# Six gated-map buffers for five, eleven kept gelu results for thirteen, and the second U block split at the end of the score stage

## The chip, the cores and the metric

The kernel runs on one core of a Trainium2 chip. The metric is the device time of one execution in microseconds (us). TensorE is PE (its weight loads PEld), VectorE DVE, ScalarE ACT, GpSimd POOL, SyncE SP.

## What is computed

Two layers, each a token mixer followed by a PEER expert layer; the change lies in the expert layer. For every token and each of 8 heads, 16 of 16384 experts are picked by product keys, and the output is the sum of their V rows, weighted by gelu of the token's product with their U row, times a softmax gate.

```python
def peer_ffn(xn, wq, sub_keys, u_tab, v_tab):
    q = jnp.matmul(xt, wq).reshape(t, PEER_HEADS, 2, PEER_SUBDIM)
    scores = jnp.einsum('thcd,hcnd->thcn', q, sub_keys)
    sv, si = lax.top_k(scores, PEER_TOPK)
    ...
    best_s, best_p = lax.top_k(cand_s, PEER_TOPK)
    gate = jax.nn.softmax(best_s, axis=-1)
    ...
        act = jnp.einsum('td,thkd->thk', xb, u_tab[ib])
        wgt = jax.nn.gelu(act) * gb
        return jnp.einsum('thk,thkd->td', wgt, v_tab[ib])
```

## The kernel before

Of the 512 tokens, 384 are computed densely: U is cut into 128 blocks of 128 experts, and all products of a block with the 384 tokens are made on PE. The last 128 tokens take their rows by indirect DMAs on POOL (`gather`, one row per token and step, followed by one multiply on DVE, L743 or L754).

A U block `e` passes these steps: `uload` (DMA of 512 KB into one of three `u_raw`), `uprep` (ACT rounds it to the upper half `u_hi`, L688), `uprep_lo` (DVE subtracts to get the lower half `u_lo`, L682; three buffers of each half), and `uact` (24 matmuls, L714, of which the first two of a block need only `u_hi` and the third needs `u_lo`; then gelu on ACT, L717). `act_st` holds `NB` gelu results; the first `NS` = 60 blocks are stored to memory (`ge`), the others stay in `act_st` until the V loop uses them.

The expert layer of a layer runs in these stages; the times are those of the first layer (the second is alike, 1611.6 us later).

- **Score stage** (to 443 us): queries and key scores; its instructions are put in order by the scheduler of the framework. At its end `uprep(0)` splits U block 0.
- **Top-k stage** (448 to 574 us, `stage2`): DVE picks the 16 best of each token tile, in four tiles. From here on the code's order is the order on each engine, but for work that the scheduler finds free. `credit(0.8)` at every `yield` lets U blocks in: each whole credit emits one `uphase(e)`, which puts `u_lo` of block e+1 on DVE, `u_hi` of e+2 on ACT and the 24 matmuls of e on PE. After each tile PE transposes its indices (L868, L869).
- **Map stage** (589 to 825 us): gates are put in place by one-hot products, in 24 batches of 16 tokens. `make_maps(b, step)` makes a batch on DVE: step 0 two equality maps `oeq` (L900, two buffers), steps 1 to 3 one gated map `oag` each (L905, `AGB` buffers; a batch uses three). `quad(b, b4)` is 12 matmuls on PE (L918) that need all five maps, then ACT moves the result to `st` (L920); every eight quads `st` is stored (L922). Order of issue: quad (b, 0..3), each followed by one step of batch b+1, `credit(0.38)`, and after every third quad a gather. U blocks stop at `pace["e"] == UB - 4`, where `UB = NS + NB - 3`: at 66.
- **Seven U blocks alone** (825 to 856 us; `u_tail` = 66 to 72), with matmul banks of a new pool.
- **V loop** (856 to 1612 us): for each of 128 blocks V is split as U was, `wh`/`wl` are gelu times gate, and 18 matmuls (L1011) are added up; the U blocks left (55) are spread over the first 120 steps, and most gathers run here.

Of the kernel before, what the change touches and what calls it, by code (L numbers as in the profile page):

```python
# [41 lines left out]
NCH = TD // TC  # L42
GE = 4
GPAD = 128
NB = 13
NS = 60
UB = NS + NB - 3
W_S = 0.8
W_O = 0.38
G_R = 1  # L50
AGB = 5
UR = 3
G_B = 1
GBUF = 4
# [15 lines left out]
def trunk_kernel(ctx: ExitStack, tc: tile.TileContext, x, norm1_g, w_in, sb_qn_g, sb_kn_g, ml_conv_w,  # L70
# [598 lines left out]
    def layer(l):  # L669
        with ExitStack() as pctx:  # L670
            pools = {}
            uraw, uT, vraw, vT, wT, g4 = {}, {}, {}, {}, {}, {}

            def uload(e):
                if e < NK:
                    uraw[e] = pools["up"].tile([P, ND, P], F32, name="u_raw", bufs=UR)
                    nc.sync.dma_start(uraw[e], peer_ut[l, e])

            def uprep_lo(e):
                if e in uraw:  # L680
                    src = uraw.pop(e)
                    nc.vector.tensor_sub(uT[e][1], src, uT[e][0].bitcast(F32))  # L682

            def uprep(e, lo=True):
                if e < NK:
                    uh = pools["up"].tile([P, ND, P], F32R, name="u_hi", bufs=3)
                    ul = pools["up"].tile([P, ND, P], F32R, name="u_lo", bufs=3)
                    nc.scalar.activation(uh, uraw[e], AF.Copy)  # L688
                    uT[e] = (uh, ul)
                    if lo:  # L690
                        uprep_lo(e)

            with ExitStack() as fctx:
                ps = fctx.enter_context(tc.tile_pool(name="ps_f", bufs=1, space=PSUM))
                wst = fctx.enter_context(tc.tile_pool(name="wst", bufs=1))
                mctx = ExitStack()
                fr = mctx.enter_context(tc.tile_pool(name="fr", bufs=1))
                at = mctx.enter_context(tc.tile_pool(name="at", bufs=1))
                mixing(l, wst, fr, at, ps)
                pr, xg, sbuf, svs, sis = peer_front(l, pctx, mctx, at, wst, ps, pools, uload)  # L700
                uprep(0)
            dr = pctx.enter_context(tc.tile_pool(name="dr", bufs=1, space=bass.MemoryType.DRAM))
            gd = dr.tile([NCH, P, NK * TC + GPAD], F32, name="gd")
            ge = dr.tile([NS, P, TD], F32, name="ge")
            gb = pctx.enter_context(tc.tile_pool(name="gb", bufs=GBUF - 2))
            act_st = pctx.enter_context(tc.tile_pool(name="act_st", bufs=NB))
            gelu = {}
# [13 lines left out]
            def uphase(e, ps):  # L721
                uprep_lo(e + 1)
                uload(e + 4)
                uprep(e + 2, lo=False)
                uact(e, ps)
# [34 lines left out]
            def gather(n):  # L760
                for f, p in [todo.pop() for _ in range(min(n, len(todo)))]:
                    f(p)
# [8 lines left out]
            with ExitStack() as bctx:  # L771
# [117 lines left out]
                def pairs(row, b):  # L889
                    row = row[:, b * OT:(b + 1) * OT].rearrange("p (q b) -> p q b", b=2)  # L890
                    return row[:, :, None, :].to_broadcast(QS)

                def make_maps(b, step):
                    if b >= n_bat:
                        return
                    if step == 0:
                        eq = oh.tile([P, 2] + QS[1:], BF16, name="oeq")
                        maps[b] = (eq, [])
                        for i in range(2):
                            nc.vector.tensor_tensor(eq[:, i], iota_t[:, None].to_broadcast(QS), pairs(idxT[:, i], b),  # L900
                                                    op=ALU.is_equal)
                    else:
                        eq, ag = maps[b]
                        ag.append(oh.tile(QS, BF16, name="oag", bufs=AGB))
                        nc.vector.tensor_mul(ag[-1], eq[:, 0], pairs(gateT[:, step - 1], b))  # L905

                def quad(b, b4):
                    c, o = divmod(b * OT, TC)
                    o += b4 * 4
                    if o == 0:  # L910
                        sts[c] = stg.tile([P, NK, TC], F32, name="st")
                    st = sts[c]
                    eq, ag = maps[b]
                    pg = ps.tile([P, 4, NK], F32, name="oh", bufs=5)
                    for k in range(4):
                        q, r = divmod(b4 * 4 + k, 2)
                        for i in range(3):
                            nc.tensor.matmul(pg[:, k, :], eq[:, 1, q, :, r], ag[i][:, q, :, r],  # L918
                                             start=(i == 0), stop=(i == 2))
                    nc.scalar.activation(st[:, :, o:o + 4].rearrange("p i t -> p t i"), pg, AF.Copy)  # L920
                    if o + 4 == TC:
                        nc.scalar.dma_start(gd[c, :, :NK * TC], sts.pop(c).rearrange("p i t -> p (i t)"))  # L922
                    if b4 == QB - 1:
                        del maps[b]

                def credit(w):
                    pace["credit"] += w
                    while pace["credit"] >= 1 and pace["e"] < UB - 4:
                        uphase(pace["e"], ps)
                        pace["e"] += 1  # L930
                        pace["credit"] -= 1

                with tc.manual_schedule():
                    uprep(1, lo=False)
                    uload(3)
                    for t in (NT - 1, *range(NT - 1)):
                        for _ in stage2(t):
                            credit(W_S)
                    casts = [f() for f in late]
                    credit(W_S)  # L940
                    for f in casts:
                        f()
                    tkctx.close()
                    with ExitStack() as octx:
                        oh = octx.enter_context(tc.tile_pool(name="oh", bufs=2))
                        stg = octx.enter_context(tc.tile_pool(name="stg", bufs=2))
                        for step in range(4):
                            make_maps(0, step)
                            credit(W_O)
                        for b in range(n_bat):  # L950
                            for b4 in range(QB):
                                quad(b, b4)
                                make_maps(b + 1, b4)
                                credit(W_O)
                                gather((b * QB + b4) % 3 == 1)
                u_tail = pace["e"]

            with ExitStack() as cctx:
# [12 lines left out]
                def vload(k):  # L971
                    if k >= NK:
                        return
                    e = order[k]
                    if e < NS:
                        gelu[e] = vp.tile([P, TD], F32, name="gelu_r", bufs=3)
                        nc.sync.dma_start(gelu[e], ge[e])
                    if e % GE == 0:
                        g4[e // GE] = vp.tile([P, NCH, GE, TC], F32, name="gt4")
                        nc.sync.dma_start(g4[e // GE].rearrange("p c i t -> p c (i t)"),  # L980
                                          gd[:, :, e * TC:(e + GE) * TC].rearrange("c p f -> p c f"))
                    vraw[e] = vp.tile([P, D], F32, name="v_raw", bufs=3)
                    nc.sync.dma_start(vraw[e], peer_v[l, e * NK:(e + 1) * NK, :])
# [30 lines left out]
                with tc.manual_schedule():  # L1014
# [11 lines left out]
                    for k in range(NK):  # L1026
                        u_on = eu < NK and (k + 1) * (NK - NS - NB) >= (eu - NS - NB + 1) * UEND
                        vload(k + 2)
# [15 lines left out]
    for l in range(depth):  # L1044
        layer(l)
# [36 lines left out]
```

## Time and profile before

| | |
|---|---|
| runs, us | 3225.39, 3228.98 (median), 3235.2 |
| profiled execution, us | 3232.74, of which the span 3231.0 |
| busy in the span | PE 96%, PEld 86%, DVE 78%, ACT 43%, POOL 21% |
| granted TensorE clock, mean | 0.986 of full speed |
| moved by DMA | 748.49 MB, 232 GB/s in the mean |

The span runs from the first to the last instruction; 1.7 us of the execution lie around it. PE is near its limit in every stage, so what matters are the stretches in which it stands still: 3231.0 - 3116.7 = 114.3 us in all.

### The profile page before, as it was taken

Reading aid. Unit: us, or ns where it says so; the run is one execution under the profiler, and the core shown is the slowest. Engines: PE = TensorE matmul, PEld = TensorE weight load, DVE = VectorE, ACT = ScalarE, POOL = GpSimd, SP = SyncE. Lnnn points to the kernel's source line nnn. Section 1 sums busy time; section 2 is a strip of 40 time slices with the busy share of each in tenths; the row PEclk is TensorE's granted clock in tenths of the full one; section 3 lists DMA queues with packets and bytes.
Section 4 is the critical chain, followed back from the end, with each engine's and each line's share of the span. In section 5 each row is a group of like instructions: output and inputs, shape, how many; then the busy total and the mean of one; then the engine's idle time right before and its main releaser. Section 6 shows DMA issues by size and latency. Waiting matters only on the chain.

```text
span 3231.0 us, 46311 instructions
## 1 busy us (share of the span) xinstructions
PE 3116.7 (96%) x17496; PEld 2776.7 (86%) x17496; DVE 2509.5 (78%) x4655; ACT 1388.0 (43%) x2002; POOL 681.5 (21%) x563
## 2 busy tenths in 40 slices
PE   8999999999999999999989999999999999999999
PEld 8877889998888888888887878899988888888888
DVE  4757889988677777877747578899886777778777
ACT  4553424566433333333355533345663333333333
POOL 1000000122233333333300000001212333333333
PEclk9999999999999999999999999999999999999999
DMA  4212325687999999999732123257879999999997
GB/s 141 68 33 61 102 70 176 232 291 264 337 331 324 324 332 316 334 330 323 252 107 67 34 60 101 75 186 242 289 262 322 328 329 321 332 318 336 328 324 264
DMA packets 329344, 748.49 MB, mean 232 GB/s; under 512 B 26404, under 2 KB 191328, under 8 KB 326048
## 3 DMA queue, kind: packets, MB, share of 16 engines
q1 hardware_dynamic: 233632, 401.76, 37.3%
q0 software_dynamic: 74752, 269.84, 23.9%
q10 hardware_dynamic: 20736, 73.93, 6.0%
q8 instruction: 137, 2.24, 0.3%
q14 instruction: 87, 0.71, 0.1%
HBM read 669.41 MB, written 76.02 MB: 231 GB/s over the span
## 4 chain that ended last, share of the span: by engine, by line
PE 85%; DVE 10%; ACT 3%; issue 2%; DMA 1%; SPq 0%; ACTq 0%; POOL 0%; DVEq 0%; POOLq 0%
PE y L1011 32%; PE act L714 26%; PE mm L187 13%; PE oh L918 4%; PE mm L533 3%; DVE u_lo L682 2%; DVE oag L905 1%; PE zz L367 1%; PE zz L653 1%; PE zz L467 1%; PE y L400 1%; PE y L478 1%; PE zz L392 1%; DVE bp L808 1%; DVE bp L805 1%
## 5 line engine op out<-in xcount | busy, mean ns | idle before, releaser
L714 PE MATMUL act<-xh,u_hi 128*128 128x384 f32 x2048 | 699.5, 342 | 6.4 <-ACT st L920 5.1
L714 PE MATMUL act<-xh,u_lo 128*128 128x384 f32 x2048 | 693.1, 338 | 11.2 <-DVE u_lo L682 11.2
L714 PE MATMUL act<-xl,u_hi 128*128 128x384 f32 x2048 | 693.0, 338 | 0.0
L1011 PE MATMUL y<-v_hi,wh 128*128 128x512 f32 x1536 | 599.9, 391 | 3.9 <-ACT wh L998 3.9
L1011 PE MATMUL y<-v_lo,wh 128*128 128x512 f32 x1536 | 599.6, 390 | 0.7 <-DVE v_lo L999 0.7
L1011 PE MATMUL y<-v_hi,wl 128*128 128x512 f32 x1536 | 598.7, 390 | 0.0
L997 ACT ACTIVATE v_hi<-v_raw 128x1024 fp32r<-128x1024 f32 x256 | 272.0, 1063 | 648.0 <-issue 575.5
L682 DVE TENSOR_TENSOR u_lo<-u_raw,u_hi 128x1024 fp32r<-128x1024 f32 x256 | 312.3, 1220 | 182.8 <-ACT u_hi L688 182.7
L999 DVE TENSOR_TENSOR v_lo<-v_raw,v_hi 128x1024 fp32r<-128x1024 f32 x256 | 312.9, 1222 | 160.8 <-ACT v_hi L997 160.8
L714 PEld LDWEIGHTS act<-xh,u_lo 128*128 128x128 f32 x2048 | 387.3, 189 | 13.6 <-DVE u_lo L682 13.3
L714 PEld LDWEIGHTS act<-xh,u_hi 128*128 128x128 f32 x2048 | 387.4, 189 | 11.4 <-ACT st L920 5.4
L714 PEld LDWEIGHTS act<-xl,u_hi 128*128 128x128 f32 x2048 | 387.2, 189 | 4.1
L740 POOL DMA_INDIRECT sbuf<-in_peer_u_dram,idx x128 | 170.8, 1334 | 1012.8 <-DVE sbuf L743 482.1
L717 ACT ACTIVATE gelu<-act 128x384 f32<-128x384 f32 x256 | 126.1, 492 | 521.7 <-PE act L714 521.6
L1011 PEld LDWEIGHTS y<-v_hi,wl 128*128 128x128 f32 x1536 | 289.2, 188 | 61.5 <-DVE wl L1000 0.7
L1011 PEld LDWEIGHTS y<-v_hi,wh 128*128 128x128 f32 x1536 | 288.8, 188 | 60.9 <-ACT wh L998 4.5
L1011 PEld LDWEIGHTS y<-v_lo,wh 128*128 128x128 f32 x1536 | 289.1, 188 | 57.0 <-DVE v_lo L999 1.3
L688 ACT ACTIVATE u_hi<-u_raw 128x1024 fp32r<-128x1024 f32 x256 | 271.7, 1062 | 37.0 <-ACT gelu L717 7.7
L740 POOL DMA_INDIRECT rows<-in_peer_u_dram,idx x128 | 165.5, 1293 | 365.9 <-DVE rows L743 354.1
L751 POOL DMA_INDIRECT sbuf<-in_peer_v_dram,idx x128 | 167.7, 1311 | 279.6 <-DVE x_sb L754 262.6
L920 ACT ACTIVATE st<-oh 128x512 f32<-128x512 f32 x192 | 198.6, 1141 | 46.6 <-PE oh L918 46.6
L751 POOL DMA_INDIRECT rows<-in_peer_v_dram,idx x128 | 159.3, 1245 | 280.0 <-DVE x_sb L754 246.4
(295 smaller groups left out, 5158.7 us busy)
## 6 DMA issues: line engine op xcount, KB each, us to landing
u_raw<-in_peer_ut_dram SPq DMA_DIRECT2D x256, 512.0 KB, 5.0
v_raw<-in_peer_v_dram SPq DMA_DIRECT2D x256, 512.0 KB, 6.5
gd<-st ACTq DMA_DIRECT2D x24, 2048.0 KB, 8.0
gt<-gd SPq DMA_DIRECT2D x64, 768.0 KB, 9.4
ge<-gelu ACTq DMA_DIRECT2D x120, 192.0 KB, 3.8
gelu_r<-ge SPq DMA_DIRECT2D x120, 192.0 KB, 6.1
w_raw<-in_w_in_dram SPq DMA_DIRECT2D x28, 768.0 KB, 4.4
w_raw<-in_peer_wq_dram SPq DMA_DIRECT2D x20, 768.0 KB, 5.5
```

What stands on the lines that cost most here:

```text
L187: nc.tensor.matmul(ps, a_sel(a[ah], d), b_sel(b[bh], d), start=(d == 0 and i == 0), stop=(d == n - 1 and i == 2))
L682: nc.vector.tensor_sub(uT[e][1], src, uT[e][0].bitcast(F32))
L688: nc.scalar.activation(uh, uraw[e], AF.Copy)
L714: nc.tensor.matmul(pa[:, :TD], a[:, d, :], b[:, d, :TD], start=(d == 0 and i == 0), stop=(d == ND - 1 and i == 2))
L717: nc.scalar.activation(gelu[e], pa[:, :TD], AF.Gelu_apprx_tanh)
L740: nc.gpsimd.indirect_dma_start(out=r, out_offset=None, in_=u_rows, in_offset=bass.IndirectOffsetOnAxis(ap=idx[:, p:p + 1], axis=0))
L751: nc.gpsimd.indirect_dma_start(out=r, out_offset=None, in_=v_rows, in_offset=bass.IndirectOffsetOnAxis(ap=idx[:, p:p + 1], axis=0))
L918: nc.tensor.matmul(pg[:, k, :], eq[:, 1, q, :, r], ag[i][:, q, :, r], start=(i == 0), stop=(i == 2))
L920: nc.scalar.activation(st[:, :, o:o + 4].rearrange("p i t -> p t i"), pg, AF.Copy)
L997: nc.scalar.activation(vh, vraw[e], AF.Copy)
L999: nc.vector.tensor_sub(vl, vraw.pop(e), vh.bitcast(F32))
L1011: nc.tensor.matmul(ya[2 * t + half], a[:, tsl], b[:, hs], start=(k == 0 and i == 0), stop=(k == NK - 1 and i == 2))
```

## The change

```diff
-NB = 13
+NB = 11
...
-AGB = 5
+AGB = 6
...
             def uprep_lo(e):
-                if e in uraw:
+                if e in uraw and e in uT:
...
                 pr, xg, sbuf, svs, sis = peer_front(l, pctx, mctx, at, wst, ps, pools, uload)
                 uprep(0)
+                uprep(1)
...
                 with tc.manual_schedule():
-                    uprep(1, lo=False)
                     uload(3)
```

A gated map takes 4 KB of a partition and a gelu result 1.5 KB. With `NB` = 11, `UB` is 68 for 70: U blocks in the map stage stop at 64, the seven alone are 64 to 70, and 57 stand in the V loop. The lower half of U block 1 is made in the score stage; the changed condition keeps `uphase(0)` from making it again. From line 702 to 934 the changed kernel's line numbers are one higher.

Three places show what moves. The first is DVE near the end of the norm that opens the score stage (`rs` is the row scale of a tile, `xg` the normed last tile, `xl` the lower half of its transpose), as a piece of the difference:

```order
 L682 TENSOR_TENSOR u_lo<-u_raw,u_hi 128x1024
 L151 SCALAR_TENSOR_TENSOR rs<-rq_b,rs 128x1
+L682 TENSOR_TENSOR u_lo<-u_raw,u_hi 128x1024
 L214 SCALAR_TENSOR_TENSOR xg<-x_sb,rs,sp 128x1024
 L203 TENSOR_TENSOR xl<-zz,xh 128x4x128
```

The lower half of block 1 now stands between the last row scale and `xg`. The second place is DVE in the first tile of the top-k stage (the searches of heads, `bs` and `bp` their values and places), before:

```order
L807 MAX bs<-c_3914 128x8
L808 MAX_INDEX bp<-bs,c_3914 128x8
L682 TENSOR_TENSOR u_lo<-u_raw,u_hi 128x1024
L804 MAX bs<-cand 128x8
L805 MAX_INDEX bp<-bs,cand 128x8
```

and now:

```order
L808 MAX bs<-c_3915 128x8
L809 MAX_INDEX bp<-bs,c_3915 128x8
L805 MAX bs<-cand 128x8
L806 MAX_INDEX bp<-bs,cand 128x8
L807 MATCH_REPLACE c_3954<-bs,cand 128x64
```

That lower half is gone from between the second and the third head; all later ones keep their places. The third place is the end of the map stage. On ACT each `st` row is one quad and each `gelu` one U block; the last rows of the first layer's map stage before:

```order
L920 ACTIVATE st<-oh 128x4x128 x3
L688 ACTIVATE u_hi<-u_raw 128x1024
L717 ACTIVATE gelu<-act 128x384
L920 ACTIVATE st<-oh 128x4x128
L922 DMA gd<-st 128x4096
L920 ACTIVATE st<-oh 128x4x128 x2
L688 ACTIVATE u_hi<-u_raw 128x1024
L717 ACTIVATE gelu<-act 128x384
L920 ACTIVATE st<-oh 128x4x128 x2
L688 ACTIVATE u_hi<-u_raw 128x1024 x2
L717 ACTIVATE gelu<-act 128x384
L920 ACTIVATE st<-oh 128x4x128 x4
```

and now:

```order
L921 ACTIVATE st<-oh 128x4x128 x3
L688 ACTIVATE u_hi<-u_raw 128x1024 x2
L718 ACTIVATE gelu<-act 128x384
L921 ACTIVATE st<-oh 128x4x128
L923 DMA gd<-st 128x4096
L921 ACTIVATE st<-oh 128x4x128 x8
L923 DMA gd<-st 128x4096
```

Four quads stood behind the last U block of the stage, and now nine do. On DVE the same place, with the last batch's maps, reads now:

```order
L906 TENSOR_TENSOR oag<-oeq,gateT 128x2048
L682 TENSOR_TENSOR u_lo<-u_raw,u_hi 128x1024
L901 TENSOR_TENSOR oeq<-iota_t,idxT 128x2048 x2
L744 SCALAR_TENSOR_TENSOR sbuf,act_g<-sbuf,xg 128x1024
L906 TENSOR_TENSOR oag<-oeq,gateT 128x2048 x3
L744 SCALAR_TENSOR_TENSOR rows,act_g<-rows,xg 128x1024 x2
```

The last batch's two equality maps, a gather's multiply and its three gated maps follow each other with no lower half between them.

## Rows read from the trace of the kernel before

**Rows 1.** The page, busy us (share of the span) xinstructions of each engine.
```profile
PE 3116.7 (96%) x17496; PEld 2776.7 (86%) x17496; DVE 2509.5 (78%) x4655; ACT 1388.0 (43%) x2002; POOL 681.5 (21%) x563
```
**Rows 2.** The page, the chain that ended last, shares by engine.
```profile
PE 85%; DVE 10%; ACT 3%; issue 2%; DMA 1%; SPq 0%; ACTq 0%; POOL 0%; DVEq 0%; POOLq 0%
```
**Rows 3.** Waits of PE, both layers: us in total, times, longest us.
```profile
PE oh L918 <- DVE oag L905: 32.2, 28, 1.9
PE act L714 <- DVE u_lo L682: 11.2, 6, 4.8
```
**Rows 4.** Stages: us, busy PE, PEld, DVE, ACT, POOL (xinstructions), PEclk, DMA, GB/s.
```profile
448.00:574.00 126.00, 118.00 (x654) 116.07 (x654) 120.56 (x417) 55.15 (x69) 4.06 (x4) 0.97 0.56 176
...
589.00:825.00 236.00, 217.88 (x1994) 210.37 (x1992) 208.41 (x215) 149.04 (x168) 52.65 (x33) 1.00 0.78 273
825.00:856.00 31.00, 29.39 (x168) 29.07 (x168) 14.69 (x19) 10.26 (x16) 5.87 (x7) 1.00 1.00 367
856.00:1612.00 756.00, 755.13 (x3623) 663.77 (x3624) 597.50 (x748) 271.46 (x365) 269.47 (x214) 1.00 0.92 319
```
**Rows 5.** Timeline of a batch's end: start, us, what [idle before <-releaser]; DVE.
```profile
635.23 1.23 DVE L905 TENSOR_TENSOR oag<-oeq,gateT 128x2048 bf16<-128x2048 bf16 x1 [2.05 <-PE oh L918]
...
637.52 2.36 DVE L900 TENSOR_TENSOR oeq<-iota_t,idxT 128x2048 bf16<-128x2048 bf16 x2
```
**Rows 6.** The same timeline, PE.
```profile
636.51 0.73 PE L918 MATMUL oh<-oag,oeq 128*128 128x128 bf16 x10 [1.09 <-DVE oag L905]
```
**Rows 7.** Map stage, DVE groups: xcount | busy us, mean ns | idle before, releaser.
```profile
L905 DVE TENSOR_TENSOR oag<-oeq,gateT 128x2048 bf16<-128x2048 bf16 x68 | 82.3, 1221 | 26.6 <-PE oh L918 26.6
L900 DVE TENSOR_TENSOR oeq<-iota_t,idxT 128x2048 bf16<-128x2048 bf16 x44 | 51.8, 1219 | 0.0
L682 DVE TENSOR_TENSOR u_lo<-u_raw,u_hi 128x1024 fp32r<-128x1024 f32 x37 | 45.0, 1219 | 0.0
L743 DVE SCALAR_TENSOR_TENSOR sbuf<-sbuf,xg 128x1024 f32<-128x1024 f32 x16 | 19.5, 1218 | 0.0
```
**Rows 8.** The chain that ended last, 440 to 600 us: start, us, what.
```profile
451.94 1.12 DVE u_lo L682
...
591.36 4.29 PE act L714 x24
```
**Rows 9.** End of the map stage on PE, in order of time.
```profile
820.03 2.93 PE L918 MATMUL oh<-oag,oeq 128*128 128x128 bf16 x48
825.19 0.44 PE L714 MATMUL act<-xh,u_hi 128*128 128x384 f32 x1 [2.23 <-ACT st L920]
```
**Rows 10.** Start of the top-k stage on PE.
```profile
453.12 0.69 PE L714 MATMUL act<-xh,u_lo 128*128 128x384 f32 x1 [4.79 <-DVE u_lo L682]
```
**Rows 11.** The second lower half of the top-k stage on DVE.
```profile
455.47 1.20 DVE L682 TENSOR_TENSOR u_lo<-u_raw,u_hi 128x1024 fp32r<-128x1024 f32 x1
```
**Rows 12.** End of the top-k stage on PE.
```profile
574.02 0.41 PE L868 MATMUL tr<-ident,ii 128*128 128x128 f32 x2 [1.62 <-DVE ii L852]
```
**Rows 13.** Waits of DVE from 443 to 596 us: us in total, times, longest.
```profile
DVE sbuf L661 <- ACT sc L656: 1.4, 1, 1.4
```
**Rows 14.** Score stage, the last tile's norm on DVE.
```profile
336.09 1.28 DVE L214 SCALAR_TENSOR_TENSOR xg<-x_sb,rs,sp 128x1024 f32<-128x1024 f32 x1
```
**Rows 15.** Score stage, its transposes on PE.
```profile
339.26 0.60 PE L199 MATMUL zz<-ident,xg 128*128 128x128 f32 x4
```
**Rows 16.** Stretches after PE stood still; columns as in Rows 4.
```profile
453.10:458.70 5.60, 5.58 (x17) 5.58 (x18) 5.22 (x31) 0.00 (x0) 0.00 (x0) 0.50 0.49 124
825.10:828.50 3.40, 3.31 (x19) 3.31 (x20) 0.00 (x0) 0.04 (x1) 0.07 (x1) 1.00 1.03 299
2346.40:2349.80 3.40, 3.40 (x18) 3.40 (x17) 3.40 (x4) 1.95 (x2) 0.65 (x1) 0.50 0.83 257
2438.50:2441.90 3.40, 3.40 (x13) 3.40 (x12) 0.00 (x0) 0.00 (x0) 0.00 (x0) 0.51 1.07 341
```
**Rows 17.** V loop, a PE group: columns as in Rows 7.
```profile
L1011 PE MATMUL y<-v_hi,wh 128*128 128x512 f32 x768 | 299.9, 391 | 1.9 <-ACT wh L998 1.9
```

## The prediction

> **What bounds the kernel now.** I read the page first. PE is busy for 96% of the span [rows 1], and the chain that ended last runs through PE for 85% of it and through DVE for 10% [rows 2]. So there is little to win but the stretches in which PE stands still, and a change can win only those that it touches. The waits of PE name two such: its one-hot products wait for gated maps of DVE, 32.2 us in 28 waits, 14 in each layer, and its U blocks wait for lower halves, 11.2 us in 6, the longest 4.8 [rows 3]. The table by stage then says who has room. In the map stage PE is busy for 217.88 of 236 us and DVE for 208.41; in the V loop PE is busy for 755.13 of 756 [rows 4], so a U block that is moved there takes its own time and no more, and none is gained. In the top-k stage DVE is busy for 120.56 of 126 us.
>
> **The sixth map buffer.** The timeline of one batch's end shows what it touches. DVE stands still for 2.05 us until PE has ended a quad, then makes a gated map in 1.23 us [rows 5]; PE, which has finished that quad, stands still for 1.09 us until this map is there [rows 6]. With five buffers a batch's third map takes the buffer of the first map of the batch before, which is read until that batch's last quad; so its multiply can start only when PE has nothing left but quads that need it. DVE has 26.6 us of idle time in the map stage, all of it before gated maps and waiting for PE, none before equality maps or lower halves [rows 7]. With six the third map takes a buffer that was free a batch earlier, and this wait of both is gone: 32.2/2 = 16.1 us per layer.
>
> What is late next is DVE itself. It starts operations 1.13 us apart (two equality maps take 2.36, one alone 1.22 [rows 5, 7]). A batch is five maps, 1.52 lower halves at 1.12 [rows 8] and 1.33 gathers at 1.22 [rows 7]: 5.65 + 1.7 + 1.6 = 9.0 us. On PE a batch is four quads, 2.93 us with the last one's run-out and 2.75 without [rows 9], and 1.52 U blocks of 4.29 [rows 8]: 9.3 us. So PE stays the longer by a little, but a batch with one U block is 7.0 us on PE and 8 to 9 on DVE, and the lead that DVE may have is one batch, since equality maps have two buffers. The longest of the 14 waits is 1.9 us [rows 3], 0.8 above the common 1.09: there DVE was late by itself. I leave two waits of 1 us in each layer, 2.0 us; the bounds are none and half of the 16.1.
>
> **Eleven gelu results.** U blocks in the map stage end at 64 for 66, and nine quads stand behind the last one for four. While the last batch but one is in the quads, DVE has to make the last batch's maps, and cannot start before quad 3 of the batch ahead of it is done, because the two equality maps are in use till then. DVE then needs five maps and a gather's multiply, 5 x 1.13 + 1.22 = 6.9 us; PE has four quads, 2.75. Before, two U blocks of 4.29 stood in this place and hid it. PE now stands still for 6.9 - 2.75 = 4.1 us per layer; without the gather it would be 2.9, with a second one ahead of the last map 5.3. The wait of 2.23 us behind the last quad for ACT to empty the matmul banks [rows 9] stays. Behind it seven U blocks follow in both kernels, and in front of the V loop the 1.9 us for `wh` [rows 17] stays too. The two U blocks go into the V loop at their own length. There a kept gelu result is used four or more V blocks after it is made, and its buffer was freed two or more blocks earlier, by the order of groups; so PE waits for neither.
>
> **The lower half of block 1.** PE waits 4.79 us for it at 453 us [rows 10]. Yet what it costs is not what it gives back. The lower half of block 2 ends 3.6 us behind that of block 1 [rows 8, 11], so the wait moves to block 2, and then DVE is the bound: from 443 to 596 us DVE waits once, 1.4 us for the last scores, ahead of the top-k stage [rows 13], and at the stage's end PE waits 1.62 us for the indices [rows 12]. So the top-k stage ends when DVE is through, and it gets shorter by the DVE time that leaves it, 1.12 us per layer [rows 8]. The upper bound is the wait and the half-rate stretch behind it, some 2.5 us, if that reached the end.
>
> Where the operation goes it is hidden: it delays `xg`, which ended at 336.09 + 1.28 = 337.4 us [rows 14], by 1.12, and PE's transposes began at 339.26 [rows 15], 1.9 us behind it; the scheduler also puts six matmuls ahead of them. On SP's queue the load of U block 4 now waits for this lower half ahead of the first key loads, which so go out some 1.1 us later. I take 0 for both; if the cover were gone it would be 1.1 us per layer.
>
> **The clock.** After PE stood still for 4.79 us its granted clock was 0.50 of full, the lower of its two levels, to 458.7 us; after 2.23 us at the map stage's end it was 1.00 in the first layer; in the second layer it was 0.51 for 3.4 us behind the same place, and 0.50 for 3.4 us inside the map stage [rows 16]. Such a stretch costs at most half of its 3.4 us, 1.7. With 4.1 us of standing still I expect one at each map stage's end, which the second layer pays already, and none inside: 1.5 for the first layer, 1.0 for a longer one somewhere, less 1.5, so +1.0. The Trainium skill ("TensorE: Matmul & The Clock Gate", section "HAM oscillation — how this bites in real kernels") says that a PE which waits between bursts falls back to the low clock and pays for it again after each wait. The trace agrees for the wait of 4.79 us, and shows after the 2.23 us that it is not certain for a short one.
>
> **The sum.** -32.2 + 2 x 2.0 + 2 x 4.1 - 2 x 1.12 + 1.0 = -21.2 us. The profiled execution took 3232.7 us (span 3231.0 and 1.7 around it), so it would take 3211.5. The median of the runs is 3.8 lower than the profiled one, so the median after is 3229.0 - 21.2 = 3207.8, rounded to 3208.
>
> **The rivals.** *DVE becomes the bound of the map stage.* For it speaks that DVE is within 10 us of PE there [rows 4]. Then half of the 32.2 stays: 16.1 for the 4.0, a change of -9.1, 3220 us.
>
> *The low clock answers every new stop.* The stop before the last batch drops PE to half rate through the last quads and the first U blocks, two stretches of 1.7 us lost in each layer, and once more in the middle of each map stage: +10 for the +1.0, 3217 us. For it speak the 0.50 after 4.79 us [rows 16]; against it, the map stage of the first layer held 1.00 throughout, with 14 waits [rows 4]. It is what the rule of "TensorE: Matmul & The Clock Gate" in the Trainium skill, taken at its word, would make of this kernel.
>
> *The early lower half gives all that PE lost.* That is 4.79 + 2.5 us per layer for 1.12: -33.6, 3195 us. Against it stands that DVE never waits in the stage [rows 13].
>
> *Slower: the sixth buffer frees nothing.* If the third map's multiply waits for the batch before it in any case, because two equality buffers let DVE no further ahead, the 32.2 stay and only the stops at the two map stages' ends are new: +8.2 - 2.2 + 1.0 to 4.0, so 7 to 10 us slower, 3236 to 3239 us. It decides if DVE's idle time in front of gated maps stays at 26 us a layer. Against it: no equality map waited [rows 7].
>
> **How the numbers follow.** The forecast has a chance of 0.70, with a range of its own from 3200 (no waits left, no slow stretch) to 3216 (waits of 4 us left in each layer and a longer stop). The bound by DVE has 0.11, the clock 0.08, the early half 0.06, the slower case 0.05. The range of 8 in 10 is 3198 to 3220: below it the full early half, above it the slower case and about half of the bound by DVE. 0.3% is 9.7 us, about what a measurement tells from no change; faster than 3219.3 are the forecast, the early half, most of the clock and a part of the DVE case, 0.85; the same, 0.12; slower by as much, 0.03.
>
> **What would show it.** The waits of PE for gated maps fall from 28 to some 8, and from 32.2 to about 12 us, of which one of about 4 us stands just ahead of the last four quads of each layer. DVE's idle time before gated maps falls from 26.6 to under 10 us per layer, besides the one before the last batch. The wait of 4.79 us is gone, one of about 3 us stands at block 2, the wait for the indices at the stage's end stays, and the map stage begins 1.1 us earlier. The V loop of a layer is longer by two U blocks. Wrong would be: waits for gated maps still in every second batch; a stop at the end that is over 6 us or missing; PE waits inside the V loop, where there is now none above 2 us.

## The result and the profile after

The changed kernel takes 3206.43 us in the median of four runs (3197.81 to 3208.66), the one before 3228.47 of four: a ratio of 0.993, 95% interval 0.9914 to 0.9946. It is 22 us faster, clear of the 0.3% that a measurement tells from nothing, and 1.6 us from the 3208 predicted.

The profiled execution is the fastest of the four: 3197.81 us, span 3195.9, which is 35.1 below the span of before. Not all of that is the change. By the first matmul of U block 0 in each layer, the mixers and score stages took 443.5 and 442.5 us before, and 440.9 and 437.3 in this execution, 7.8 us less for the same work but one U block's halves in each, with a mean granted clock of 0.98 and 0.97 for 0.97 and 0.96 in those stretches. The other three executions ran at a mean clock of 0.984 to 0.985 over the whole span and took 3205.8 to 3208.7 us, this one at 0.987. So the two profiles are compared by stages, from the first matmul of U block 0 on.

The stages of the first layer of the changed kernel, from the table by stretches (columns as in [rows 4]):

```profile
445.00:570.00 125.00, 118.73 (x656) 115.90 (x655) 119.53 (x416) 54.72 (x69) 4.05 (x4) 0.97 0.53 172
586.00:802.00 216.00, 209.11 (x1935) 202.80 (x1933) 204.65 (x213) 145.81 (x163) 52.03 (x33) 0.99 0.82 293
802.00:833.00 31.00, 29.16 (x168) 28.84 (x167) 15.02 (x20) 10.54 (x16) 6.55 (x7) 1.00 0.98 364
833.00:1598.00 765.00, 764.19 (x3672) 672.31 (x3672) 600.76 (x751) 273.99 (x369) 265.02 (x216) 1.00 0.92 317
```

The map stage has become 20 us shorter, of which two U blocks of some 4.2 us are work that went away; the V loop has become 8 to 9 us longer, which is these two blocks. The top-k stage and the U blocks alone are as before within 1.1 us, and PE is still busy through the whole V loop. The waits of PE in both layers say where the rest came from (us in total, times, longest):

```profile
PE oh L919 <- DVE oag L906: 11.5, 10, 2.0
...
PE act L715 <- DVE u_lo L682: 7.6, 6, 3.1
...
PE act L715 <- ACT st L921: 2.2, 2, 1.1
```

The waits for gated maps, 32.2 us in 28 before [rows 3], are 11.5 in 10. The waits behind the last quads are 2.2 us, where the kernel before has

```profile
PE act L714 <- ACT st L920: 5.1, 2, 2.8
```

The groups of DVE in the first layer's map stage show the other side (xcount | busy, mean ns | idle before, releaser):

```profile
L906 DVE TENSOR_TENSOR oag<-oeq,gateT 128x2048 bf16<-128x2048 bf16 x68 | 81.3, 1220 | 0.0
L901 DVE TENSOR_TENSOR oeq<-iota_t,idxT 128x2048 bf16<-128x2048 bf16 x44 | 51.9, 1222 | 10.1 <-PE oh L919 10.1
```

DVE never waits before a gated map now, where it waited 26.6 us [rows 7]; it waits 10.1 us before equality maps, a step earlier in the batch, and so has them ready. Each operation takes what it took.

The end of the stage is where eleven gelu results show. First PE, then DVE, in order of time:

```profile
788.41 3.62 PE L919 MATMUL oh<-oag,oeq 128*128 128x128 bf16 x60
794.01 0.23 PE L919 MATMUL oh<-oag,oeq 128*128 128x128 bf16 x1 [1.99 <-DVE oag L906]
795.14 0.22 PE L919 MATMUL oh<-oag,oeq 128*128 128x128 bf16 x1 [0.90 <-DVE oag L906]
796.27 4.37 PE L919 MATMUL oh<-oag,oeq 128*128 128x128 bf16 x46 [0.92 <-DVE oag L906]
...
801.76 0.45 PE L715 MATMUL act<-xh,u_hi 128*128 128x384 f32 x1 [1.11 <-ACT st L921]
```
```profile
789.31 2.36 DVE L901 TENSOR_TENSOR oeq<-iota_t,idxT 128x2048 bf16<-128x2048 bf16 x2
791.59 1.22 DVE L744 SCALAR_TENSOR_TENSOR sbuf<-sbuf,xg 128x1024 f32<-128x1024 f32 x1
...
792.73 3.49 DVE L906 TENSOR_TENSOR oag<-oeq,gateT 128x2048 bf16<-128x2048 bf16 x3
```

PE runs five quads (60 matmuls) and then stands at each of the last batch's three gated maps in turn: 1.99 + 0.90 + 0.92 = 3.81 us, while DVE makes two equality maps, a gather's multiply and the three maps one behind the other. The last 46 matmuls take 4.37 us; before, 48 took 2.93 [rows 9]. The table by stretches has the reason (796.8 to 800.1, and the first U blocks behind it):

```profile
796.80:800.10 3.30, 3.30 (x34) 3.30 (x32) 3.30 (x6) 2.59 (x3) 2.16 (x2) 0.50 0.64 197
801.80:805.20 3.40, 3.40 (x20) 3.40 (x21) 0.00 (x0) 0.00 (x0) 0.94 (x1) 1.00 1.02 357
```

The granted clock was 0.50 there, the lower level, after the stop, and full again when the U blocks began. The wait for ACT behind the last quads is 1.11 us and no more 2.23: ACT can catch up in the stop and keep up with slower quads. Which of the two counts for more, no run separates.

In the top-k stage the wait moved to block 2, and the wait for the indices at the stage's end is what it was [rows 12] (PE):

```profile
452.94 0.69 PE L715 MATMUL act<-xh,u_lo 128*128 128x384 f32 x1 [3.08 <-DVE u_lo L682]
```
```profile
570.23 0.41 PE L869 MATMUL tr<-ident,ii 128*128 128x128 f32 x2 [1.57 <-DVE ii L853]
```

### The profile page after: what moved, and what is told of

Read it like the earlier page. It is cut to its first block, busy times and chain, and to the rows that moved or that the text cites. A ratio compares the mean times of both kernels' runs of the same rounds, so it can differ in the third digit from the quotient of the medians.

```text
span 3195.9 us, 46339 instructions
## 1 busy us (share of the span) xinstructions
PE 3109.0 (97%) x17496; PEld 2771.2 (87%) x17496; DVE 2508.0 (78%) x4655; ACT 1387.7 (43%) x2002; POOL 677.6 (21%) x563
## 5 line engine op out<-in xcount | busy, mean ns | idle before, releaser
L752 POOL DMA_INDIRECT rows<-in_peer_v_dram,idx x128 | 165.8, 1295 | 299.0 <-DVE x_sb L755 262.3
L752 POOL DMA_INDIRECT sbuf<-in_peer_v_dram,idx x128 | 157.7, 1232 | 277.5 <-DVE x_sb L755 261.6
```

The lines of the kernel that those rows point to most:

```text
L752: nc.gpsimd.indirect_dma_start(out=r, out_offset=None, in_=v_rows, in_offset=bass.IndirectOffsetOnAxis(ap=idx[:, p:p + 1], axis=0))
```

## The experiments

All are timed against the kernel before on the same chip: the first four in one set (before: 3227.00 us, median of 21), the last four in another (3225.25, median of 9).

**The sixth buffer with 13 gelu results.** There is no room for it as it stands, so the equality map that only DVE reads becomes a tile of its own with one buffer.

```diff
-AGB = 5
+AGB = 6
+EQB = 2
...
-                        eq = oh.tile([P, 2] + QS[1:], BF16, name="oeq")
+                        eq = [oh.tile(QS, BF16, name=f"oeq{i}", bufs=(1, EQB)[i]) for i in range(2)]
```

> The sixth gated-map buffer alone, on the kernel before: 13 gelu results, no early lower half. To make room, the equality map that only DVE reads is a tile of its own with one buffer (the one that PE reads keeps two). Theory: all 28 waits of PE for gated maps go, and with 13 results there is no stop at the map stage's end: 14 to 16 us less per layer, 28 to 32 us in all, about 3197 us, and next to no wait of PE for gated maps. Rival 'DVE becomes the bound': half of the waits stays, about -16. Rival 'the gain came from the early lower half or from elsewhere': no change.

Measured: 3189.52 us, ratio 0.9888 (0.9873 to 0.9903). In the first layer's map stage PE waits for nothing but ACT, once, behind the last quad:

```profile
PE act L715 <- ACT st L921: 3.4, 1, 3.4
```

All 14 waits are gone and PE is not stopped by DVE at all, so DVE is not the next bound at this distribution of U blocks. The time fell by 37.5 us, more than the 32.2 of the waits. The first layer's map stage shows one reason: from its first quad to the end of its last, PE has the same work in both kernels. First before, where the last quads end at 822.96 us [rows 9], then here, with the table by stretches last:

```profile
589.12 2.24 PE L918 MATMUL oh<-oag,oeq 128*128 128x128 bf16 x36
```
```profile
585.10 2.24 PE L919 MATMUL oh<-oag,oeq 128*128 128x128 bf16 x36
...
797.56 2.93 PE L919 MATMUL oh<-oag,oeq 128*128 128x128 bf16 x48
```
```profile
589.00:804.00 215.00, 211.63 (x1948) 205.96 (x1947) 205.81 (x212) 145.97 (x165) 52.63 (x33) 1.00 0.85 301
```

That is 233.8 us before and 215.4 now, both at a granted clock of 1.00: 18.4 us for 14 waits that add up to 16.1 (half of the 32.2), so a wait costs some 0.17 us beyond its idle time. By estimate this is the run-out of the last matmul before it: one that runs alone is busy for 0.22 or 0.23 us (the rows at 794.01 and 795.14 above), while 60 in a row took 3.62, 0.06 each. For 28 waits it comes to 4.7 us. The wait for ACT behind the last quads grew by 1.6 us in both layers together, to 6.7, and there is one half-rate stretch less in the expert layers of this profile, at most 1.7 us. One reservation: with one buffer for the first equality map, DVE may start a batch one operation earlier than with two paired ones, so this is the sixth buffer and a little more lead.

**Eleven gelu results alone.**

```diff
-NB = 13
+NB = 11
```

> Eleven gelu results alone, on the kernel before, with five gated-map buffers. Theory: PE stands still for 4 us more ahead of the last batch in each layer, and for about 1 us less behind the last quad, so +5 to +8 us, about 3235 us; the 14 waits per layer stay. Rival 'eleven cost nothing': 0. Rival 'the V loop or the moved U blocks pay as well': more than +10.

Measured: 3234.94 us, ratio 1.0027 (1.0018 to 1.0037), +8 us. The waits of PE:

```profile
PE oh L918 <- DVE oag L905: 39.3, 34, 1.9
...
PE act L714 <- ACT st L920: 2.2, 2, 1.1
```

7.1 us more than before at three maps per layer, 2.9 less behind the last quads. The last quads at half rate (46 matmuls in 4.06 and 4.00 us, where 48 took 2.93) and the run-outs of six more waits bring some 3.4 us more, by estimate. The V loop is longer by two U blocks and nothing else. So the part costs what the theory says, at the upper edge of it.

**The early lower half alone**, with the changed condition of `uprep_lo`.

```diff
...
                 uprep(0)
+                uprep(1)
...
-                    uprep(1, lo=False)
```

> The early lower half of U block 1 alone, on the kernel before. Theory: the top-k stage is DVE's, so 1.1 us per layer, -2.2 us in all, within what can be told from nothing; the wait of 4.8 us gives way to one of about 3 us for block 2. Rival 'all that PE lost comes back': 7.3 us per layer, -14.6. Rival 'xg is delayed and PE waits for it': +2.

Measured: 3228.24 us, ratio 1.0001 (0.9992 to 1.001). The profile has the wait of 3.1 us in place of 4.8 and no other new wait:

```profile
PE oh L919 <- DVE oag L906: 32.1, 28, 1.9
...
PE act L715 <- DVE u_lo L682: 8.3, 8, 3.1
```

From U block 0 to the last transposes the top-k stage took 130.4 and 130.9 us in its two layers, for 131.5 and 131.5 before; the changed kernel has 130.4 in both. So the 1.1 us per layer is there at the stage's end; that PE lost 4.8 us was no loss of the kernel, for DVE set the pace. The half-rate stretch behind that wait was not won back either: 6.8 us at the lower level follow the wait of 3.1 us too (from 456.1 us).

Yet little of the 1.1 us is left at the first quad, for PE's clock falls once more, behind the wait for the indices. The stretches just after the last transposes in the two layers, before and then here (columns as in [rows 4]):

```profile
574.80:578.20 3.40, 3.40 (x12) 3.40 (x13) 3.26 (x7) 0.00 (x0) 0.00 (x0) 0.51 0.43 112
2186.10:2189.50 3.40, 3.15 (x19) 3.15 (x20) 3.26 (x8) 0.06 (x1) 0.00 (x0) 1.00 0.41 84
```
```profile
575.60:579.00 3.40, 3.40 (x12) 3.40 (x12) 3.26 (x8) 0.00 (x0) 0.00 (x0) 0.50 0.54 156
2186.70:2190.10 3.40, 3.40 (x12) 3.40 (x11) 3.26 (x8) 0.00 (x0) 0.00 (x0) 0.50 0.44 137
```

The last transposes and the first quads of the second layer, before and here:

```profile
2186.35 0.33 PE L869 MATMUL tr<-ident,gt 128*128 128x128 f32 x1 [0.26 <-DVE gt L856]
...
2199.00 2.24 PE L918 MATMUL oh<-oag,oeq 128*128 128x128 bf16 x36
```
```profile
2186.34 0.33 PE L870 MATMUL tr<-ident,gt 128*128 128x128 f32 x1 [0.26 <-DVE gt L857]
...
2200.56 2.24 PE L919 MATMUL oh<-oag,oeq 128*128 128x128 bf16 x36
```

That is 12.65 us before and 14.22 here, 1.6 more. In all twelve layers profiled with the early lower half (this kernel, the changed one and the experiments below that have it) the stretch is there, and 14.2 to 14.4 us pass; of the eight without it (before, the first, second and fifth experiment) only the first layer of before has it, with 14.4 us, and the others take 12.7 to 12.9. So from U block 0 to the first quad all but that one of the layers without the early half take 143.8 to 144.1 us, those with it 144.2 to 144.8: by the profiles this part wins nothing, and the time shows no gain either. Why the clock falls there with this edit, no run shows.

**U blocks to 66 with eleven results**, in the changed kernel.

```diff
-                    while pace["credit"] >= 1 and pace["e"] < UB - 4:
+                    while pace["credit"] >= 1 and pace["e"] < UB - 2:
```

> The changed kernel with the U blocks of the map stage stopped at 66 again (so 66 in the map stage, five alone in place of seven, 57 in the V loop). Theory: the stop of 3.8 us ahead of the last batch of each layer was the price of stopping at 64, and goes, while the wait behind the last quad grows again by 1 us: -5 to -6 us against the changed kernel, about 3201 us. Rival 'five blocks alone do not cover the loads of the V loop': PE waits for wh at the V loop's start by 8 us more in each layer, and the time is that of the changed kernel or above.

Measured: 3196.10 us, ratio 0.9899 (0.9884 to 0.9914), against 0.993 of the changed kernel: some 9 us less, where 5 to 6 were expected, with intervals of some 5 us to either side on both. By the two profiles it is 2.4 and 1.9 us less in the two layers from U block 0 to the V loop (389.8 and 390.0 us for 392.2 and 392.0). The waits of PE from 586 to 831 us:

```profile
PE act L715 <- ACT st L921: 2.6, 1, 2.6
PE y L1011 <- ACT wh L998: 1.9, 1, 1.9
PE oh L919 <- DVE oag L906: 1.9, 2, 1.0
```

The stop ahead of the last batch is gone, the two waits in the middle of the stage are left, and five blocks alone cover the loads of the V loop as seven do: the wait for `wh` is the old 1.9 us [rows 17]. The wait behind the last quad has grown from 1.11 to 2.6 us, a little more than the 1 us expected.

**Four gated-map buffers**, on the kernel before.

```diff
-AGB = 5
+AGB = 4
```

> Four gated-map buffers on the kernel before, nothing else changed. Theory that a map's multiply waits for the batch before it to leave its buffer: now the second and the third map of a batch both wait, so PE stands still in each of those ends for two multiplies in place of one, and in some batches that had no wait: 25 to 30 us more per layer, +50 to +60 in all, about 3282 us. Rival 'DVE sets the map stage's pace whatever the buffers are': within 5 us of before.

Measured: 3316.29 us, ratio 1.0277 (1.0261 to 1.0293), +91 us where 50 to 60 were expected. The waits, in both layers, and then the map stage of the first (columns as in [rows 4]):

```profile
PE oh L918 <- DVE oag L905: 85.0, 56, 3.2
```
```profile
573.50:866.00 292.50, 247.69 (x2066) 238.42 (x2065) 222.63 (x231) 151.75 (x172) 48.16 (x33) 0.94 0.66 226
```

The waits grew by 52.8 us, as expected, and doubled in number: the theory of the buffers holds in both directions. The rest is mostly the clock, 0.94 of full in the first layer's map stage where it was 1.00 [rows 4]. After a wait of 3.20 us the U block's matmuls run thus:

```profile
621.25 1.22 PE L918 MATMUL oh<-oag,oeq 128*128 128x128 bf16 x10 [3.20 <-DVE oag L905]
622.23 0.67 PE L714 MATMUL act<-xh,u_hi 128*128 128x384 f32 x1
622.69 0.52 PE L714 MATMUL act<-xl,u_hi 128*128 128x384 f32 x1
...
624.17 0.34 PE L714 MATMUL act<-xh,u_hi 128*128 128x384 f32 x1
```

At 0.52 us and 0.32 apart they are at the lower level, and at 0.34 at the upper one. From the first quad to the last the two layers took 43.6 and 46.1 us more than before; 26.4 us of each are waits, and the run-outs of 14 more waits, at 0.17 us, some 2.4. That leaves 15 and 17 us to the clock; a mean of 0.94 over 292 us would lose 6% of it, about 17 us, if PE were never idle.

**The 64 U blocks spread to the stage's end**, in the changed kernel.

```diff
-W_O = 0.38
+W_O = 0.35
```

> The changed kernel with the same 64 U blocks of the map stage spread to its end (credit of 0.35 for 0.38 by each quad). Theory that DVE is the next bound: the stop ahead of the last batch goes, but batches with one U block are more frequent and PE waits for DVE in them, some 5 to 7 us of short waits per layer, so the time is that of the changed kernel within 3 us. Rival 'only the place of the U blocks is at fault': -8 us, like the kernel that stops at 66.

Measured: 3205.30 us, ratio 0.9937 (0.9923 to 0.9951), the time of the changed kernel. PE waits, in both layers:

```profile
PE oh L919 <- DVE oag L906: 14.9, 16, 1.0
```

None of them is over 1.0 us: the stop at the end is gone, and more short waits take its place, as expected. But the reason given was too simple, for DVE waits as well (first layer's map stage):

```profile
DVE oeq L901 <- PE oh L919: 7.3, 7, 2.9
DVE u_lo L682 <- ACT u_hi L688: 5.0, 2, 3.5
...
```

It stands ahead of equality maps until PE frees their two buffers, and twice for an upper half of ACT. So DVE has time left in the stage, and what is short in these batches may be its lead; the last experiment tests that for the two waits that the fourth experiment keeps.

**The sixth buffer, 13 results and the early lower half.** The first experiment's tiles in the changed kernel, with

```diff
-NB = 11
+NB = 13
```

> The sixth gated-map buffer with 13 gelu results (the single-buffered equality map makes the room) and the early lower half: the first experiment's kernel and the third's edit together. Theory: -2 us against the first experiment, 3187 us, not to be told from it; about 19 us below the changed kernel. Rival 'the early lower half costs something now that the map stage is shorter': above 3192.

Measured: 3190.94 us, ratio 0.9895 (0.9879 to 0.991). At 34.3 us below its before, for 37.5, it is not to be told from the first experiment, and it lies between the theory's 3187 us and the rival's 3192, so the time decides for neither. By the profiles the early lower half gives nothing here either: the top-k stages are 1.2 and 0.7 us shorter than the first experiment's, and 14.2 us for 12.9 and 12.7 pass from the last transposes to the first quad.

**Three buffers for the equality map that PE reads, U blocks to 66.** The tiles of the first experiment with `EQB = 3`, six gated maps, eleven results, `UB - 2`.

> The changed kernel with U blocks stopped at 66 and the equality maps split: one buffer for the one that only DVE reads, three for the one that PE reads, same memory. Theory: DVE may now lead by two of five maps more, so the two waits of 1 us that the changed kernel keeps in the middle of each map stage go: 3192 us, 4 below the kernel that stops at 66. Rival 'these waits are DVE's own lateness, which buffers do not cure': equal to that kernel, 3196.

Measured: 3191.93 us, ratio 0.9895 (0.988 to 0.991). From 589 to 812 us PE waits once, behind the last quad:

```profile
PE act L716 <- ACT st L922: 3.3, 1, 3.3
```

The two waits in the middle are gone, in the second layer too, so they were a matter of how far DVE may lead and not of its own lateness. The time alone does not show it: 0.9895 against 0.9899 of the kernel that stops at 66, where the theory had 4 us, 0.0012. By the profiles the layers took 387.4 and 387.9 us from U block 0 to the V loop, for 389.8 and 390.0, 4.6 us less in all.

## Why the prediction was right

**The sixth buffer.** The step that names the cause held: in the changed kernel DVE has no idle time before gated maps, and with four buffers PE waits 53 us more. The term still left something out: it counted the idle time alone, and 18 waits less are, at the first experiment's 0.17 us, another 3.1 us. What was left as two waits of 1 us per layer is 1.0 and 0.9 us, 5.7 less the 3.8 at the end. The rival that DVE becomes the bound would have left half of the 32.2; 11.5 are left, and 7.6 of these are the other term.

**Eleven results.** 4.1 us per layer was forecast for the stop ahead of the last batch, 3.81 is there. That the wait of 2.23 us behind the last quad stays was wrong: it is 1.11, and in both layers 2.2 us for 5.1. Alone the part costs 8 us, where the sum had 8.2 and 1.0 for the clock.

**The lower half.** 1.12 us per layer was forecast, 1.1 is there at the end of the top-k stage, and the wait at block 2 is 3.08 us where "about 3" was expected. In the score stage `xg` starts 1.2 us behind the last row scale's start, and PE reaches its transposes 1.5 us after it has ended; no wait for a key load is among the waits of PE. So the cost of zero held (DVE, then PE):

```profile
333.61 0.15 DVE L151 SCALAR_TENSOR_TENSOR rs<-rq_b,rs 128x1 f32<-128x1 f32 x1
333.68 1.22 DVE L682 TENSOR_TENSOR u_lo<-u_raw,u_hi 128x1024 fp32r<-128x1024 f32 x1
334.82 1.28 DVE L214 SCALAR_TENSOR_TENSOR xg<-x_sb,rs,sp 128x1024 f32<-128x1024 f32 x1
```
```profile
337.62 0.61 PE L199 MATMUL zz<-ident,xg 128*128 128x128 f32 x4
```

What the prediction left out is the half-rate stretch behind the wait for the indices, which the third experiment shows with this edit in both layers. It had the map stage begin 1.1 us earlier; counted from U block 0 the first quad comes 1.3 us earlier in the first layer, where before had such a stretch as well, and 0.5 us later in the second. So this term of the sum, 2.2 us, is not a gain that can be kept.

**The clock** came out near its +1.0 in the sum, but not in its places. The low clock does follow the new stop in both layers, yet it falls on the last quads (some 1.5 us in each layer: 46 matmuls take 4.37 us, where 48 took 2.93); the U blocks behind, for which the prediction counted 1.5 to 2.5 us, run at full clock. None falls in the middle of a map stage, as the rival had it. The half-rate stretches that the second layer had inside its map stage and in the U blocks behind it [rows 16] are gone in this profile, and one behind the wait for the indices (1.6 us) is new there. That is an estimated 3.0 + 1.6 us, less at most 3.4.

**The sum.** By the two profiles the first layer from U block 0 to the V loop took 413.0 us before and 392.2 now, the second 415.2 and 392.0; with the two U blocks that moved, 8.5 and 8.4 us longer in the V loops, this is -12.3 and -14.8 us, -27 in all, where the sum was -21.2. Two terms that the sum held at nothing make up the 6 us, by estimate: the waits for ACT behind the last quads (-2.9) and the run-outs of 18 waits (-3.1). The median changed by -22. That it lies within 1.6 us of the forecast is in part luck: the executions scatter over 11 us, and -27 is within the interval of the ratio. Which of the two is the truer mean is left open.

**The forecasts of sign.** The slower rival fell with DVE's idle time; the early half's full 33.6 us fell with the third experiment. The 28 us that the three parts have by themselves (-37.5, +7.9, +1.2) are more than the 22 of the change; the first experiment's lead of one more operation, which spares it the two waits per layer that the changed kernel keeps, is 3.9 us of that (the last experiment shows that a longer lead removes them), and the intervals cover the rest.

The fastest kernels are the first, seventh and eighth experiment at 3190 to 3192 us, 1.1% below the kernel before: six gated-map buffers, the equality map split in two tiles, and no stop at the map stage's end. Without the split, the fourth is at 3196 us.

## What to carry to other kernels

Where two engines wait for each other in turn at the same place in a loop, count the buffers that pass between them against what one round needs: five for three per round was one short, and both stood still for it. Before a removed wait is counted as gain, ask which engine sets the end of that stage; here a wait of 4.8 us on the busiest engine was worth 1.1 at the stage's end, because another one had next to no idle time in the whole stage, and a stretch at the lower clock behind it took that back. A wait that does count costs more than its idle time: 14 waits of 16.1 us were worth 18.4. Memory for a buffer is paid for somewhere: the two results given up cost 8 us at the end of a stage, and splitting a tile of which one half needs no second buffer got the same memory at no cost that the runs show.

## What the runs showed of the hardware

In the kernel before, the second and the third experiment a map stage has 13 waits of PE of 1.1 us and one of 1.9 us (the second experiment's has the stop at its end besides). Behind the short ones the clock stayed at its upper level in all six stages; behind the one of 1.9 us it fell in three of the six, for 3.4 us [rows 16]. With four buffers there were 28 in a stage, 1.5 us in the mean and 3.2 at most; the granted clock of the first layer's map stage fell from 1.00 to 0.94, and 53 us more of waiting cost 91. And the executions of the changed kernel differ together with the granted clock: 3197.8 us at a mean of 0.987, 3205.8 to 3208.7 at 0.984 to 0.985, though its instructions are the same.
